# Loading the first half of w_o one block per product, and scaling all of w_ffn_down on VectorE

## The chip, the core and the metric

The kernel runs on one core of one Trainium2 chip. The core has a matrix engine (TensorE; PE in the profile, its weight loads PEld), three engines for elementwise work (VectorE, or DVE; ScalarE, or ACT; GpSimd, or POOL) and SyncE (SP), which here only issues DMAs. Each engine takes its instructions strictly in the order in which they were written, and waits on semaphores for the others. The metric is the device time of one execution in microseconds; the median of several runs is what is compared.

## The reference

One block of a network over 1024 latent tokens of width 1024 and 256 context tokens, batch 1, in fp32: a two-way mLSTM branch and a grouped-query attention branch on the same normed input, their gated merge, and a SwiGLU. Cut to what matters here:

```python
def merge_branches(zg, ym, ya, w_pa, w_pb, w_o):
    g_m, g_a = jnp.split(jax.nn.sigmoid(zg), N_BRANCH, axis=-1)
    return (g_m * (ym @ w_pa) + g_a * (ya @ w_pb)) @ w_o

def swiglu(h, w_g, w_u, w_d):
    return (jax.nn.silu(h @ w_g) * (h @ w_u)) @ w_d

def reference(x, ...):
    ...
    x = x + g1 * y                  # y is merge_branches' result
    x = x + g2 * swiglu(rmsnorm(x, norm2_g[l]) * (1.0 + sc2) + sh2, w_ffn_gate[l], w_ffn_up[l], w_ffn_down[l])
    return rmsnorm(x, final_g)
```

The gates g1 and g2 are vectors over the 1024 output columns. The kernel multiplies them into the columns of w_o and of w_ffn_down.

## The kernel before

Every fp32 product is made from three matmuls (mm3, L104 to L106): each operand is first split into a high part (`split`, L98, ScalarE) and a low part, what the high part leaves (L99, on GpSimd, or on VectorE where the call says so). A block of weights therefore passes a load (L129, issued by SP), in some cases a scaling (L131, VectorE), L98 and L99 before PE can use it.

Buffers of 4 KB per partition ("s" in the profile, and `s_` with a number where instructions are listed) come from one list that hands out the buffer that has been free longest. A load into a buffer waits for the last user of the buffer.

**From w_pb to w_o.** The loop over n (eight, KT) multiplies each 128 columns of w_pb with the attention output, for two halves of the tokens: 24 matmuls to a product. VectorE evicts each product from PSUM (L1426 and L1427; their inputs, the gate and the other branch, are loaded into tile t at L1420 and L1421), and ScalarE and GpSimd split it into mT, the operand of the next products. `load_o(b, js)` loads, scales and splits blocks j of the column half b of w_o. Then come the products with w_o: for two halves of the tokens, two column halves b, four token tiles t, 24 matmuls each. The order of the instructions on every queue is that of the text, except where the scheduler of the program moves an instruction with others of its place. Products have five PSUM banks here.

**Down projection.** w_ffn_down is multiplied in five groups of two blocks, by a Strassen scheme with seven products to a group (`ORDER`: n = 1, 2, 6, 7, 5, 4, 3). Group 0 is a set alone, groups 1 and 2 are the second, 3 and 4 the third set; within a set a product is accumulated in PSUM over its groups, four PSUM banks to a product (q = 0 to 3), eight banks in all. `down_load` issues the loads of a step five steps ahead, `down_prep` makes the operands two steps ahead: the four blocks (a, b) of the weights are scaled by the gate (`scaled`, L1685), combined (`minus`, L1688), and split. When a product is complete, its four banks are evicted, by ScalarE (L1789) for group 0 with n = 1, 6, 7, else by VectorE, which adds to an accumulator (L1791). L1766 adds accumulators at the end.

Of the kernel before, what the change touches and what calls it, by code (L numbers as in the profile page):

```python
# [19 lines left out]
KT = D // P  # L20
# [67 lines left out]
class Block:  # L88
# [1078 lines left out]
    def run(self):  # L1167
        nc, tc, io = self.nc, self.tc, self.io
# [33 lines left out]
        def PS(tags, name):  # L1202

            turn[tags] = i = turn.get(tags, -1) + 1
            tag = tags[i % len(tags)]
            return psum.tile([P, 512], F32, name=name, tag=tag, bufs={"X": 3, "K": 2, "Y": 2, "Z": 1}[tag])
# [15 lines left out]
        slots = self.slots = Slots()  # L1222
# [181 lines left out]
        gbc = slots.get([P, D], F32)  # L1404
        nc.sync.dma_start(gbc, self.d_g[0:1, :].partition_broadcast(P))
        w_o = {}

        def load_o(b, js):

            for j in js:  # L1410
                w_o[b, j] = self.load_s(slots, io["w_o"], 2 * j, 2, b * 512, 512, scale=gbc, lo_eng=nc.gpsimd if j % 2 else nc.vector)

        for n in range(KT):
            if n + 2 < KT:
                w_pb.append(self.load_s(slots, io["w_pb"], 0, KT, (n + 2) * P, P))
            w = w_pb[n]
            for half in range(2):
                hs = slice(half * 512, (half + 1) * 512)
                t = slots.get([P, 2, 512], F32)
                nc.sync.dma_start(t[:, 0], self.d_sm[D + n * P:D + (n + 1) * P, hs])  # L1420
                nc.sync.dma_start(t[:, 1], self.d_ms[n * P:(n + 1) * P, hs])  # L1421
                o = PS(self.acc, "pj")
                for k in range(KT):
                    y = yq[half][k // 2]
                    self.mm3(o, (w[0][:, k], w[1][:, k]), (y[0][:, k % 2], y[1][:, k % 2]), k == 0, k == KT - 1)
                nc.vector.tensor_tensor(t[:, 0], o, t[:, 0], op=ALU.mult)  # L1426
                nc.vector.tensor_tensor(t[:, 0], t[:, 0], t[:, 1], op=ALU.add)  # L1427
                hi, lo = mT[half][n // 2]
                self.split(hi[:, n % 2], lo[:, n % 2], t[:, 0])
                slots.put(t)  # L1430
            slots.put(*w)
            if n >= KT - 2:
                load_o(0, (0, 1) if n == KT - 2 else (2, 3))
        for half in range(2):
            for q in range(4):
                slots.put(*yq[half][q])
# [83 lines left out]
        for half in range(2):  # L1520
# [5 lines left out]
            if not half:  # L1526
                load_o(1, range(4))
# [142 lines left out]
        def down_prep(i, n):  # L1670

            if i == len(groups):
                ops = [slots.get([P, D], F32R) for e in range(4)]
                x, r = down[i, "a", n], down[i, "w", n]
                nc.vector.tensor_tensor(r, r, gbc, op=ALU.mult)
                self.split(ops[0], ops[1], x.rearrange("p a b -> p (a b)"))
                self.split(ops[2], ops[3], r, nc.vector)
                slots.put(x, r)
                down[i, n] = ops
                return  # L1680
            m = len(groups[i])

            def scaled(a, b, eng):
                r = down[i, a, b]
                eng.tensor_tensor(r, r, gbc[:, None, b * 512:(b + 1) * 512].broadcast_to([P, m, 512]), op=ALU.mult)  # L1685

            def minus(out, a, b, eng=nc.vector):
                eng.tensor_tensor(out, a, b, op=ALU.subtract)  # L1688

            if n == 1:  # L1690
                scaled(0, 0, nc.vector)
            elif n == 2:
                scaled(1, 0, nc.gpsimd if i else nc.vector)
            src = {1: (0, 0), 2: (1, 0), 6: (0, 0), 7: "t", 5: (0, 1), 4: (1, 0), 3: (1, 1)}[n]
            r = down[(i, src) if n == 7 else (i,) + src]
            ops = [slots.get([P, m, 512], F32R) for e in range(4)]
            self.split(ops[0], ops[1], down[i, n], nc.gpsimd if i or n not in (1, 6, 7) else nc.vector)
            self.split(ops[2], ops[3], r, nc.vector)
            if n == 2:
                r11, r12, r21, r22 = [down[i, a, b] for a in range(2) for b in range(2)]  # L1700
                scaled(0, 1, nc.vector)
                scaled(1, 1, nc.gpsimd if i else nc.vector)
                t3 = down[i, "t"] = slots.get([P, m, 512], F32)
                minus(t3, r22, r12)
                minus(r12, r12, r11)
                minus(r11, r22, r12)
                minus(r21, r21, r11, nc.gpsimd)
            slots.put(down[i, n])
            if n not in (1, 2):
                slots.put(r)  # L1710
            down[i, n] = ops

        def ahead(k, more=0):

            while at[0] < min(len(seq), k + (LOADS if k >= 0 else 3 + more) + 1):
                down_load(*seq[at[0]])
                at[0] += 1
            while at[1] < min(len(seq), k + PREPS + more + 1):
                down_prep(*seq[at[1]])
                at[1] += 1  # L1720
# [9 lines left out]
        for j in range(FP):  # L1730
# [18 lines left out]
            else:  # L1749
                self.drop_blocks("11", "21")  # L1750
                gbc = slots.get([P, D], F32)
# [141 lines left out]
```

## Time and profile before

| | us |
|---|---|
| median of 3 runs | 2277.96 |
| lowest and highest of the 3 | 2274.88 and 2279.34 |
| the profiled execution | 2284.03 |
| its span | 2282.2 |

The profile is of one execution of its own, 6.07 us above the median. The span is the part of it that the trace covers, from the first instruction to the last. Differences that are worked out from the trace are taken from the span and then set against the median. The granted TensorE clock is given in shares of full speed (2.4 GHz), and was 0.977 as a mean over the span.

### The profile page before, as it was taken

Reading aid. Unit: us, or ns where it says so; the run is one execution under the profiler, and the core shown is the slowest. Engines: PE = TensorE matmul, PEld = TensorE weight load, DVE = VectorE, ACT = ScalarE, POOL = GpSimd, SP = SyncE. Lnnn points to the kernel's source line nnn. Section 1 sums busy time; section 2 is a strip of 40 time slices with the busy share of each in tenths; the row PEclk is TensorE's granted clock in tenths of the full one; section 3 lists DMA queues with packets and bytes.
Section 4 is the critical chain, followed back from the end, with each engine's and each line's share of the span. In section 5 each row is a group of like instructions: output and inputs, shape, how many; then the busy total and the mean of one; then the engine's idle time right before and its main releaser. Section 6 shows DMA issues by size and latency. Waiting matters only on the chain. (4 is left out here: it accounts for less than half of the span.)

```text
span 2282.2 us, 29965 instructions
## 1 busy us (share of the span) xinstructions
PE 2151.4 (94%) x10875; PEld 1779.6 (78%) x10875; DVE 1529.8 (67%) x2771; ACT 980.7 (43%) x1955; POOL 906.1 (40%) x593
## 2 busy tenths in 40 slices
PE   5899999999999899999999999989799999989997
PEld 2698888988887677877877777867588888877885
DVE  4767567477879786876877786245846464667687
ACT  4534434244443564643766764124523232323343
POOL 1422222322323240302655563321554545456875
PEclk9999999999999899999999999999899999999998
DMA  7132333233323822047322224432142323274431
GB/s 263 56 89 91 109 93 106 84 97 111 98 92 105 313 76 86 11 143 254 101 77 86 84 70 137 132 130 82 47 134 94 115 91 117 94 241 144 172 102 74
DMA packets 171632, 262.40 MB, mean 115 GB/s; under 512 B 13326, under 2 KB 111702, under 8 KB 171484
## 3 DMA queue, kind: packets, MB, share of 16 engines
q1 hardware_dynamic: 161564, 236.66, 31.7%
q10 hardware_dynamic: 9920, 23.82, 2.8%
q8 instruction: 86, 1.41, 0.2%
q14 instruction: 62, 0.51, 0.1%
HBM read 190.11 MB, written 70.34 MB: 114 GB/s over the span
## 5 line engine op out<-in xcount | busy, mean ns | idle before, releaser
L99 POOL TENSOR_TENSOR s<-s,s 128x1024 fp32r<-128x1024 f32 (+1 forms) x195 | 403.9, 2084 | 670.5 <-ACT s L98 476.7
L104 PE MATMUL pr<-s,s 128*128 128x512 f32 (+1 forms) x1736 | 621.8, 360 | 19.5 <-DVE s L261 9.8
L98 ACT ACTIVATE s<-s 128x1024 fp32r<-128x1024 f32 (+2 forms) x438 | 359.4, 846 | 633.9 <-DVE s L233 80.4
L105 PE MATMUL pr<-s,s 128*128 128x512 f32 (+1 forms) x1736 | 622.5, 359 | 8.2 <-POOL s L99 5.8
L106 PE MATMUL pr<-s,s 128*128 128x512 f32 (+1 forms) x1736 | 622.1, 359 | 8.4 <-POOL s L99 4.7
L99 DVE TENSOR_TENSOR s<-s,s 128x1024 fp32r<-128x1024 f32 (+2 forms) x243 | 290.3, 1203 | 144.5 <-ACT s L98 109.8
L104 PEld LDWEIGHTS pr<-s,s 128*128 128x128 f32 x1736 | 330.4, 191 | 72.4 <-ACT s L98 13.9
L106 PEld LDWEIGHTS pr<-s,s 128*128 128x128 f32 x1736 | 330.7, 191 | 59.2 <-POOL s L99 6.4
L105 PEld LDWEIGHTS pr<-s,s 128*128 128x128 f32 x1736 | 330.9, 191 | 58.1 <-POOL s L99 6.8
L104 PE MATMUL pj<-s,s 128*128 128x512 f32 x568 | 227.4, 400 | 18.9 <-DVE s L1791 7.9
L105 PE MATMUL pj<-s,s 128*128 128x512 f32 x568 | 225.9, 398 | 4.3 <-DVE s L99 2.2
L106 PE MATMUL pj<-s,s 128*128 128x512 f32 x568 | 225.5, 397 | 1.2 <-POOL s L99 1.2
L261 DVE TENSOR_TENSOR s<-s,pr 128x512 f32<-128x512 f32 x200 | 133.1, 681 | 77.0 <-PE pr L106 72.9
L1566 DVE TENSOR_TENSOR s<-s,pr 128x512 f32<-128x512 f32 x154 | 99.6, 679 | 112.1 <-ACT s L1582 103.8
L104 PEld LDWEIGHTS pj<-s,s 128*128 128x128 f32 x568 | 109.0, 192 | 47.5 <-DVE s L1791 8.7
L1576 POOL TENSOR_TENSOR s<-s,s 128x512 f32<-128x512 f32 x44 | 70.5, 1603 | 167.8 <-ACT s L98 91.1
L1086 DVE TENSOR_TENSOR PT<-pt,PT 128x512 fp32r<-128x512 f32 (+1 forms) x192 | 112.5, 599 | 34.5 <-ACT PT L1085 32.8
L1071 ACT ACTIVATE pr<-sc,st 128x512 f32<-128x512 f32 (+1 forms) x192 | 117.8, 621 | 35.4 <-DVE st L1063 35.4
L362 POOL TENSOR_SCALAR wm<-wm,sc 128x1024 f32<-128x1024 f32 x32 | 91.2, 2849 | 103.0 <-DVE PT L1086 95.5
L105 PEld LDWEIGHTS pj<-s,s 128*128 128x128 f32 x568 | 109.4, 193 | 27.9 <-DVE s L99 3.3
L106 PEld LDWEIGHTS pj<-s,s 128*128 128x128 f32 x568 | 109.2, 192 | 25.1 <-POOL s L99 2.4
L1085 ACT ACTIVATE PT<-pt 128x512 fp32r<-128x512 f32 (+1 forms) x192 | 95.5, 525 | 66.7 <-PE pt L1082 66.0
(316 smaller groups left out, 3622.8 us busy)
## 6 DMA issues: line engine op xcount, KB each, us to landing
s<-in_w_in_dram SPq DMA_DIRECT2D x60, 512.0 KB, 3.7
d_act<-s SPq DMA_DIRECT2D x74, 256.0 KB, 2.0
s<-d_act SPq DMA_DIRECT2D x37, 512.0 KB, 4.6
wm<-in_w_mod_dram SPq DMA_DIRECT2D x32, 512.0 KB, 3.8
s<-in_w_ffn_gate_dram SPq DMA_DIRECT2D x22, 512.0 KB, 4.6
s<-in_w_ffn_up_dram SPq DMA_DIRECT2D x22, 512.0 KB, 3.9
s<-in_w_ffn_down_dram SPq DMA_DIRECT2D x22, 512.0 KB, 8.0
s<-in_w_mod_dram SPq DMA_DIRECT2D x32, 256.0 KB, 4.7
```

What stands on the lines that cost most here:

```text
L98: nc.scalar.activation(hi, src, AF.Copy)
L99: (lo_eng or nc.gpsimd).tensor_tensor(lo, src, hi.bitcast(F32), op=ALU.subtract)
L104: nc.tensor.matmul(out, lhsT=lhs[0], rhs=rhs[0], start=first, stop=False)
L105: nc.tensor.matmul(out, lhsT=lhs[0], rhs=rhs[1], start=False, stop=False)
L106: nc.tensor.matmul(out, lhsT=lhs[1], rhs=rhs[0], start=False, stop=last)
L261: eng.tensor_tensor(out, a, b, op=ALU.add)
L362: x = nc.gpsimd.tensor_scalar(loaded[i], loaded[i], self.sc[:, k, 0:1], None, op0=ALU.mult)
L1071: nc.scalar.activation(pr[:, s0:s0 + n], sc[j][:, 0:n], AF.Exp, bias=st[:, 3:4], accum_out=st[:, 4 + j:5 + j])
L1085: nc.scalar.activation(hi, src, AF.Copy)
L1086: self.pace = nc.vector.tensor_tensor(lo, src, hi.bitcast(F32), op=ALU.subtract)
L1566: nc.vector.tensor_tensor(out, a, b, op=ALU.add)
L1576: nc.gpsimd.tensor_tensor(g, g, o, op=ALU.mult)
```

## The change

It has two parts. First, the four blocks of the first column half of w_o (b = 0) are loaded one after each of the last four steps of the w_pb loop (n = 4, 5, 6, 7), where two came after n = 6 and two after n = 7; and the low parts of two of these blocks (j = 1 and 3) are made by VectorE in place of GpSimd. Second, in groups 1 to 4 of the down projection VectorE also makes the scalings of the blocks (1, 0) and (1, 1), which GpSimd made.

```diff
         def load_o(b, js):
 
             for j in js:
-                w_o[b, j] = self.load_s(slots, io["w_o"], 2 * j, 2, b * 512, 512, scale=gbc, lo_eng=nc.gpsimd if j % 2 else nc.vector)
+                w_o[b, j] = self.load_s(slots, io["w_o"], 2 * j, 2, b * 512, 512, scale=gbc, lo_eng=nc.gpsimd if b and j % 2 else nc.vector)
...
             slots.put(*w)
-            if n >= KT - 2:
-                load_o(0, (0, 1) if n == KT - 2 else (2, 3))
+            if n >= KT - 4:
+                load_o(0, (n - KT + 4,))
...
             elif n == 2:
-                scaled(1, 0, nc.gpsimd if i else nc.vector)
+                scaled(1, 0, nc.vector)
...
                 scaled(0, 1, nc.vector)
-                scaled(1, 1, nc.gpsimd if i else nc.vector)
+                scaled(1, 1, nc.vector)
```

The order of PE's instructions is the same in both kernels. Three places show what moves on the others.

VectorE, in the middle of the w_pb loop (the difference; + is the change, - is before). L1426 and L1427 are evictions: tile s_13718 is that of n = 2 and the second half of the tokens, s_13756 and s_13788 are those of n = 3. L131 and L99 with s_13967, s_13890 and s_13892 are the scalings of w_o's blocks j = 1 and j = 0 and the low part of j = 0; s_14024 is block j = 0 before:

```order
 L1426 TENSOR_TENSOR s_13718<-pj,s_13718 128x512
+L131 TENSOR_TENSOR s_13967<-s_13967,s_13538 128x1024
 L1427 TENSOR_TENSOR s_13718<-s_13718 128x512
 L1426 TENSOR_TENSOR s_13756<-pj,s_13756 128x512
 L1427 TENSOR_TENSOR s_13756<-s_13756 128x512
+L131 TENSOR_TENSOR s_13890<-s_13890,s_13538 128x1024
+L99 TENSOR_TENSOR s_13892<-s_13890,s_13891 128x1024
 L1426 TENSOR_TENSOR s_13788<-pj,s_13788 128x512
 L1427 TENSOR_TENSOR s_13788<-s_13788 128x512
-L131 TENSOR_TENSOR s_14024<-s_14024,s_13538 128x1024
```

Two scalings and a low part now stand ahead of the place where the first scaling stood before; the next two rows of the difference have block j = 2's scaling ahead of the second eviction of n = 4.

VectorE, around the last products with w_pb. First before: s_13992 is n = 6, s_14038 and s_14070 are n = 7; s_14109 is block j = 3 of the first half of w_o, s_14140, s_14147, s_14133 and s_14126 are the second half's:

```order
L1426 TENSOR_TENSOR s_13992<-pj,s_13992 128x512
L1427 TENSOR_TENSOR s_13992<-s_13992 128x512
L131 TENSOR_TENSOR s_14109<-s_14109,s_13538 128x1024
L1426 TENSOR_TENSOR s_14038<-pj,s_14038 128x512
L131 TENSOR_TENSOR s_14140<-s_14140,s_13538 128x1024
L1427 TENSOR_TENSOR s_14038<-s_14038 128x512
L131 TENSOR_TENSOR s_14147<-s_14147,s_13538 128x1024
L99 TENSOR_TENSOR s_14142<-s_14140,s_14141 128x1024
L131 TENSOR_TENSOR s_14133<-s_14133,s_13538 128x1024
L1426 TENSOR_TENSOR s_14070<-pj,s_14070 128x512
```

The same place in the change, where n = 6 is s_13974 and s_14006, and n = 7 is s_14045 and s_14077 (s_14111 is the low part of block j = 3):

```order
L131 TENSOR_TENSOR s_14109<-s_14109,s_13538 128x1024
L1426 TENSOR_TENSOR s_13974<-pj,s_13974 128x512
L1427 TENSOR_TENSOR s_13974<-s_13974 128x512
L99 TENSOR_TENSOR s_14111<-s_14109,s_14110 128x1024
L1426 TENSOR_TENSOR s_14006<-pj,s_14006 128x512
L1427 TENSOR_TENSOR s_14006<-s_14006 128x512
L131 TENSOR_TENSOR s_14133<-s_14133,s_13538 128x1024
L1426 TENSOR_TENSOR s_14045<-pj,s_14045 128x512
L1427 TENSOR_TENSOR s_14045<-s_14045 128x512
```

Block j = 3 stood behind both evictions of n = 6 and now stands ahead of both; between it and the eviction of n = 7 there is one scaling of the second half's (s_14133).

VectorE, at the down projection's second group of weights (the difference; s_18158, s_18106, s_18110 and s_18154 are the blocks (1, 0) and (1, 1) of groups 1 and 2, s_18016 is an accumulator of group 0):

```order
 L1685 TENSOR_TENSOR s_18004<-s_18004,s_17710 128x1024
 L1791 TENSOR_TENSOR s_17918<-pj,s_17918 128x512
+L1685 TENSOR_TENSOR s_18158<-s_18158,s_17710 128x1024
 L1791 TENSOR_TENSOR s_17919<-pj,s_17919 128x512 x2
+L1685 TENSOR_TENSOR s_18106<-s_18106,s_17710 128x1024
 L99 TENSOR_TENSOR s_18117<-s_17720,s_18116 128x1024
 L1685 TENSOR_TENSOR s_18108<-s_18108,s_17710 128x1024
+L1685 TENSOR_TENSOR s_18110<-s_18110,s_17710 128x1024
+L1685 TENSOR_TENSOR s_18154<-s_18154,s_17710 128x1024
 L99 TENSOR_TENSOR s_18166<-s_18004,s_18165 128x1024
 L1791 TENSOR_TENSOR s_18016<-pj,s_18016 128x512
```

Four scalings more now stand on VectorE ahead of the eviction into s_18016. GpSimd has the counterpart (the difference again):

```order
 L99 TENSOR_TENSOR s_18063<-s_17924,s_18062 128x1024
-L1685 TENSOR_TENSOR s_18158<-s_18158,s_17710 128x1024
 L99 TENSOR_TENSOR s_18115<-s_17960,s_18114 128x1024
-L1685 TENSOR_TENSOR s_18106<-s_18106,s_17710 128x1024
-L1685 TENSOR_TENSOR s_18110<-s_18110,s_17710 128x1024
-L1685 TENSOR_TENSOR s_18154<-s_18154,s_17710 128x1024
 L99 TENSOR_TENSOR s_18164<-s_18006,s_18163 128x1024
 L99 TENSOR_TENSOR s_18207<-s_18060,s_18206 128x1024
```

Three scalings in a row stood ahead of the low parts s_18164 and s_18207 there, and are gone. Groups 3 and 4 have the same later.

## Rows read from the trace of the kernel before

**Rows 1.** The page's first part: engine, busy us (share of the span) xinstructions.

```profile
PE 2151.4 (94%) x10875; PEld 1779.6 (78%) x10875; DVE 1529.8 (67%) x2771; ACT 980.7 (43%) x1955; POOL 906.1 (40%) x593
```

**Rows 2.** Windows of three stretches (columns in the first line).

```profile
core 0: us, PE busy (x) PEld busy (x) DVE busy (x) ACT busy (x) POOL busy (x), PEclk, DMA share, GB/s
...
1488.00:1503.00 15.00, 8.31 (x18) 5.18 (x18) 13.07 (x9) 4.49 (x5) 7.89 (x4) 0.66 0.69 259
2050.00:2100.00 50.00, 44.59 (x173) 35.68 (x174) 37.91 (x32) 18.98 (x25) 33.51 (x12) 0.87 0.44 157
2200.00:2240.00 40.00, 36.68 (x149) 28.93 (x148) 35.55 (x25) 11.86 (x13) 39.84 (x13) 0.92 0.15 55
```

**Rows 3.** Timeline of PE: start, us, instruction, [idle before <-releaser].

```profile
1487.78 0.39 PE L106 MATMUL pj<-s,s 128*128 128x512 f32 x1
1492.31 0.64 PE L104 MATMUL pj<-s,s 128*128 128x512 f32 x1 [4.15 <-ACT s L98]
1495.11 0.80 PE L105 MATMUL pj<-s,s 128*128 128x512 f32 x1 [2.16 <-POOL s L99]
...
1505.09 0.39 PE L106 MATMUL pj<-s,s 128*128 128x512 f32 x1
```

**Rows 4.** Timeline of VectorE from the w_pb loop to the first w_o products.

```profile
1435.22 0.69 DVE L1426 TENSOR_TENSOR s<-pj,s 128x512 f32<-128x512 f32 x1 [4.02 <-PE pj L106]
...
1440.66 0.69 DVE L1426 TENSOR_TENSOR s<-pj,s 128x512 f32<-128x512 f32 x1 [3.54 <-PE pj L106]
...
1455.09 1.22 DVE L131 TENSOR_TENSOR s<-s,s 128x1024 f32<-128x1024 f32 x1 [13.01 <-DMA s<-in_w_o_dram]
...
1481.04 1.23 DVE L131 TENSOR_TENSOR s<-s,s 128x1024 f32<-128x1024 f32 x1 [9.18 <-DMA s<-in_w_o_dram]
...
1483.45 1.23 DVE L99 TENSOR_TENSOR s<-s,s 128x1024 fp32r<-128x1024 f32 x1 [0.58 <-ACT s L98]
...
1489.89 1.23 DVE L131 TENSOR_TENSOR s<-s,s 128x1024 f32<-128x1024 f32 x1 [3.52 <-DMA s<-in_w_o_dram]
1491.04 0.68 DVE L1426 TENSOR_TENSOR s<-pj,s 128x512 f32<-128x512 f32 x1
```

**Rows 5.** Timeline of GpSimd and of SyncE's DMA issues, same place.

```profile
1492.34 2.72 POOL L99 TENSOR_TENSOR s<-s,s 128x1024 fp32r<-128x1024 f32 x1 [3.92 <-ACT s L98]
...
1476.04 19.41 SPq L129 DMA_DIRECT2D s<-in_w_o_dram  x5
```

**Rows 6.** Timeline of PE in the down projection.

```profile
2075.64 0.39 PE L106 MATMUL pj<-s,s 128*128 128x512 f32 x1
2081.06 0.80 PE L104 MATMUL pj<-s,s 128*128 128x512 f32 x1 [5.04 <-DVE s L1791]
...
2088.62 0.39 PE L106 MATMUL pj<-s,s 128*128 128x512 f32 x1
```

**Rows 7.** Timeline of VectorE in the down projection.

```profile
2057.57 1.88 DVE L1791 TENSOR_TENSOR s<-pj,s 128x512 f32<-128x512 f32 x3
...
2067.86 2.20 DVE L99 TENSOR_TENSOR s<-s,s 128x1024 fp32r<-128x1024 f32 x1 [3.51 <-issue]
...
2077.06 3.34 DVE L1688 TENSOR_TENSOR s<-s,s 128x1024 f32<-128x1024 f32 x1 [6.41 <-POOL s L99]
2080.33 0.68 DVE L1791 TENSOR_TENSOR s<-pj,s 128x512 f32<-128x512 f32 x1
```

**Rows 8.** Timeline of GpSimd and ScalarE, same stretch and the end.

```profile
2063.22 9.11 POOL L1685 TENSOR_TENSOR s<-s,s 128x1024 f32<-128x1024 f32 x3
2072.30 10.32 POOL L99 TENSOR_TENSOR s<-s,s 128x1024 fp32r<-128x1024 f32 x4
...
2194.49 5.77 POOL L99 TENSOR_TENSOR s<-s,s 128x1024 fp32r<-128x1024 f32 x2 [2.86 <-ACT s L98]
...
2068.26 1.08 ACT L98 ACTIVATE s<-s 128x1024 fp32r<-128x1024 f32 x1
```

**Rows 9.** Instructions of L1685: engine, xcount, duration ns min/median/max, starts.

```profile
L1685 DVE TENSOR_TENSOR s<-s,s x12: 1211/1221/3417, 2011.5 to 2144.0; 128x1024 f32<-128x1024 f32 x12
...
L1685 POOL TENSOR_TENSOR s<-s,s x8: 2388/3379/3409, 2056.6 to 2152.4; 128x1024 f32<-128x1024 f32 x8
```

**Rows 10.** Landing times of the loads of w_ffn_down, and PE's wait near the end.

```profile
DMA to landing us min/median/max: 4.8/8.0/9.1
...
2232.36 0.47 PE L104 MATMUL pj<-s,s 128*128 128x512 f32 x1 [2.14 <-DVE s L1791]
```

## Prediction

> **What bounds the kernel now.** The page's first part comes first: PE is busy 94% of the span, no other engine more than 67% [rows 1]. The time is PE's instructions plus PE's pauses, and a change that gives PE no work and takes none, as here, can only move pauses. So the next view is where PE pauses near the edits, by windows and then by PE's own timeline.
>
> There are three such stretches [rows 2]. From 1488 to 1503 PE is busy 8.31 of 15 us at a granted clock of 0.66, from 2050 to 2100 it is busy 44.59 of 50 at 0.87, from 2200 to 2240 36.68 of 40 at 0.92. The mean clock below 1 says that part of the stretch ran at the lower of TensorE's two levels, 1.2 in place of 2.4 GHz, so a pause costs its length and then the slow matmuls behind it.
>
> What matters first is how fast PE goes undisturbed. Two evictions in a row, each of which waited for PE, start at 1435.22 and 1440.66 [rows 4]: a product of 24 matmuls takes 5.44 us, 0.2267 us to a matmul.
>
> **The first stall.** The second of these evictions is the second half of n = 3. Counting on by 5.44, the first product of n = 7 ends at 1440.66 + 7 x 5.44 = 1478.7, the second at 1484.2. The first product with w_o gets 18 matmuls, three blocks, done by 1488.0; PE then waits 4.15 us for the high part of block j = 3 (ScalarE, L98), and one matmul on 2.16 us for its low part (GpSimd, L99) [rows 3]. What that costs is read from a matmul that runs at full pace again: the 27th after the stop, counting the one at 1492.31 as the first, starts at 1505.09 [rows 3]; undisturbed it would start at 1488.01 + 26 x 0.2267 = 1493.90. The loss is **11.2 us**.
>
> Why is block 3 late? SyncE issued the last loads of w_o from 1476.04 on [rows 5], and VectorE stands in order at the scaling of each: 13.01, 9.18 and 3.52 us of waits for the DMA [rows 4]. The product of n = 7 that PE had finished at 1478.7 was evicted at 1491.04, behind the last of these. The GpSimd low part then takes 2.72 us from 1492.34 [rows 5].
>
> **The change, first part.** The loads now come one for each of n = 4 to 7, and by the order the scaling of block 3 stands ahead of the evictions of n = 6, which PE has ready at 1467.9 and 1473.3 (1440.66 + 5 and 6 x 5.44); its low part stands between the two. Even if the load is issued only when the eviction of the product before, ready at 1462.4, is past (some 1465), lands after 5.0 us as the load issued at 1476.04 did (scaled at 1481.04), and is scaled (1.23), rounded on ScalarE (1.08, the same shape in [rows 8]) and subtracted on VectorE (1.23), it is ready by 1474. An estimate from these rows, but needed only at 1488.0: the margin is 14 us. No PSUM bank is missing meanwhile: VectorE stood still for 13.01 us before 1455.09 and PE ran on.
>
> What is late next? Ahead of the eviction of n = 7, ready at 1478.7, now stands one scaling of the second half's blocks, whose load waits for the buffer that block 3's low part frees, so about 1476 with SyncE's own 2 us. With 5.0 us it lands at 1481, the scaling ends at 1482.3, the two instructions of the eviction at 1483.7 (0.69 each), ScalarE's high part near 1484.3, and GpSimd's low part, behind a 128x1024 low part that can take 2.72, by about 1487.2 to 1488.5. The first w_o product reads it in its 21st matmul, at 1484.2 + 20 x 0.2267 = 1488.7. So it just holds, and this is the thin place: 0 to 4 us of loss may come back. I take 0, since each step of that chain is taken from a disturbed stretch and may only be shorter. Term: **-11.2 us** (bounds -11.2 to -7).
>
> Two low parts move to VectorE: 2 x 1.23 us, beside waits of 13.01 and 9.18 us that now end. They cost nothing; without that cover 2.5 us.
>
> **The second stall.** In the down projection PE stops after the matmul at 2075.64, for 5.04 us, since the next PSUM bank is evicted only by the L1791 at 2080.33 [rows 6, 7]. The 21st matmul starts at 2088.62, undisturbed at 2075.87 + 20 x 0.2267 = 2080.40: **8.2 us** lost. Ahead of that eviction VectorE stood 6.41 us before L1688, for a buffer that a GpSimd low part frees; GpSimd had run three scalings from 2063.22 for 9.11 us, then that low part as the second in a run of four from 2072.30 (10.32, 2.58 each) [rows 7, 8].
>
> **The change, second part.** Eight scalings go from GpSimd to VectorE, four of them here. On GpSimd they took 2.39 to 3.41 us each. On VectorE a scaling takes 1.21 to 3.42 [rows 9], the long ones beside a GpSimd instruction. The high part for that low part starts on ScalarE at 2068.26 and takes 1.08 [rows 8]; then GpSimd, no longer in arrears, frees the buffer at 2069.3 + 2.4 to 3.4 = 71.7 to 72.7 (all from 2000). So GpSimd is no more the last; VectorE is. Its queue, walked from the L1791 at 57.57: one eviction to 58.2; first new scaling beside GpSimd's low part, 3.42, to 61.6; two evictions to 62.9; second new scaling alone, 1.22, to 64.1; a low part to 65.3; the old scaling, alone now, to 66.5; the third and fourth new one beside GpSimd's next low parts, 3.42 each, to 73.3; a low part of 2.20 (that at 2067.86) to 75.5; an eviction to 76.1; L1688, between 1.21 and 3.34, to 78.4; and the eviction that PE waits for ends at 79.1. It ended at 81.0 before. So the stall gets 1.9 us shorter and does not go: PE still needs the bank at 75.87, and the pause of some 3 us is above the 2.14 after which PE slowed near the end [rows 10]. I take **-2 us**. Bounds: none of the four contended gives the whole -8.2 (VectorE is then at L1688 when the buffer is free, at 71.7, and PE's bank is ready at 73.6). All four contended and nothing of the waits used adds 13.7 - 6.41 = +7.3.
>
> What the trace shows here is contention: the same scaling takes 1.21 alone and 3.42 beside GpSimd, whose own takes 2.39 alone and up to 3.41 [rows 9]. The Trainium skill, in "SBUF — State Buffer", section "SBUF: two separate sides", says that VectorE with two SBUF inputs and GpSimd take turns at one port pair, each holding it for a whole instruction. The trace agrees: 3.42 is near the 1.21 + 2.39 of one behind the other. By the rule the stall stays for the most part, without it the sum would have -8.2 in place of -2.
>
> For groups 3 and 4 the same four scalings stand ahead of evictions and wait for loads, which land a median of 8.0 us after issue, 9.1 at most [rows 10]. The last of them began at 2152.4 on GpSimd [rows 9]; with 1.22 for it and 0.68 for the eviction behind it that bank is free at 2154.3. The second set begins near 2088.2, with [rows 6]; PE needs that bank after twelve products of 5.44 and 18 matmuls more (4.1), at 2157.6. With 3.3 us of slack I charge 0 (bound +4).
>
> **The end.** From 2200 to 2240 GpSimd is busy 39.84 of 40 us [rows 2], in arrears since 2194.49 [rows 8], and PE pauses there 3.32 us and loses up to 0.08 x 36.68 = 2.9 by the clock. GpSimd has no scalings left there, so the change only reaches it through an earlier start: PE comes earlier as well, so most stays. I take **-1** (bounds -6.2 and +4, as in groups 3 and 4).
>
> **The sum.** -11.2 - 2 - 1 = -14.2. Against the profiled span, 2282.2 gives 2268.0; that execution was 6.07 us above the median, so the comparison goes to the median: 2277.96 - 14.2 = 2263.8, rounded to **2264 us**.
>
> **Rivals.** B: the down projection gains nothing, since VectorE with four more instructions ends where GpSimd did, and the end neither. For it speaks that VectorE is the busier of the two (67% against 40%), and that all of its contention stays: 2277.96 - 11.2 = 2266.8. The Trainium skill's "Perfetto Trace Analysis", section "Optimizing Scalar/DVE Operations", warns of this: work moved between VectorE and GpSimd may not help, as they share a port. The trace agrees in part; GpSimd's 9.11 us in a row become at most 3.42 each on VectorE.
> C: half of the first stall comes back, through the low part of n = 7 that has 0 to 1.5 us of margin: +5.6 on mine, 2269.4. For it speaks the thin margin, against it that VectorE is out of its arrears by then.
> D: all three stalls go, for which VectorE has to run its scalings alone: -11.2 - 8.2 - 6.2 = -25.6, 2252.4. Against it speaks GpSimd at 33.51 of 50 us in that window.
> E, slower: in groups 3 and 4 VectorE, which alone evicts, stands before a scaling whose load is late. One place, the last load's scaling: each microsecond beyond the 3.3 us of slack goes to PE. To use up 14.2 and 4.6 more it would have to begin 22.1 us after 2152.4, which is more than twice the slowest landing, 9.1: the place is real, the size unlikely. At that point it gives 2282.6.
> F: nothing that can be measured, within 0.2% (4.6 us, 2273.4 to 2282.5, about what a measurement of this kernel can tell from no change): the first stall is taken over by another wait of the same size, as by an x load that a buffer holds back; 2278.
>
> **How the numbers follow.** Chances: mine 0.48 (its own range 2260 to 2267), B 0.16, C 0.12, D 0.10, F 0.09, E 0.05. The range 2252 to 2271 holds mine, B, C and about half of D. Faster 0.86, same 0.09, slower 0.05.
>
> **What would show it.** From 1400 to 1510 no PE wait over 1 us and a granted clock near 1.00; block 3's scaling on VectorE near 1470. L1685 on VectorE 20 times, on GpSimd none. The second stall, some 11 us earlier in time, still there with 3 to 4 us of pause before L1791, with VectorE busy without a break ahead of it, not waiting for GpSimd. The end still has PE waits for L1791. I am wrong if VectorE waits for a DMA at L131 or L1685 while PE waits for VectorE.

## The result, and the profile after

| | before | after |
|---|---|---|
| median of 9 runs, us | 2277.96 | 2267.21 |
| lowest and highest, us | 2269.34, 2281.53 | 2256.80, 2270.89 |
| span of the profiled execution, us | 2282.2 | 2262.3 |

The ratio of the runs is 0.9938, 95% interval 0.9924 to 0.9953: of 2277.96 us that is 14.1 us less (10.7 to 17.3). The ratio is not the quotient of the two medians: these differ by 10.75 us, at the lower end of that interval. Forecast were 14.2 less and 2264 us, 3.2 us under the median. The gains in us of the experiments below are worked out from the ratios in the same way.

The page's first part: PE's share is what it was, GpSimd has lost 30 us of work and VectorE gained 7, though it runs ten instructions more ([rows 1]); so the others take less time than before.

```profile
PE 2137.3 (94%) x10875; PEld 1772.1 (78%) x10875; DVE 1536.5 (68%) x2781; ACT 981.7 (43%) x1955; POOL 876.3 (39%) x583
```

The three stretches in windows (columns as in [rows 2]; the later ones start 10 us earlier, as PE does):

```profile
1488.00:1503.00 15.00, 14.39 (x63) 11.93 (x64) 8.70 (x7) 4.47 (x6) 4.25 (x3) 1.00 0.55 192
2040.00:2090.00 50.00, 45.89 (x197) 36.56 (x197) 45.73 (x40) 19.30 (x25) 23.62 (x9) 1.00 0.46 163
2190.00:2230.00 40.00, 37.03 (x159) 29.34 (x158) 37.68 (x26) 4.86 (x5) 35.21 (x12) 1.00 0.04 17
```

The granted clock is 1.00 in all three, where it was 0.66, 0.87 and 0.92. The second pair is not quite like with like. Before, the window opens inside another stall: PE waits 4.10 us at 2049.86 for a bank that ScalarE evicts (L1789), and its matmuls are slow up to 2056. The change has this stall too (4.18 us), but at 2037.48, ahead of its window. A window before that begins behind it has 0.93 and 186 matmuls; PE's wait before, then that window:

```profile
2049.86 0.80 PE L104 MATMUL pj<-s,s 128*128 128x512 f32 x1 [4.10 <-ACT s L1789]
```

```profile
2056.00:2106.00 50.00, 44.59 (x186) 35.91 (x185) 38.84 (x33) 17.67 (x22) 35.92 (x13) 0.93 0.38 133
```

In the second and third PE is busy hardly longer than before (45.89 against 44.59 of 50, 37.03 against 36.68 of 40), but executes more matmuls in that time (197 against 173, 159 against 149).

**The first stall.** PE's timeline at the first product with w_o:

```profile
1486.96 0.39 PE L105 MATMUL pj<-s,s 128*128 128x512 f32 x1
1488.61 0.50 PE L106 MATMUL pj<-s,s 128*128 128x512 f32 x1 [1.26 <-POOL s L99]
```

The waits for block 3 ([rows 3]) are gone; one wait of 1.26 us stands in their place, for the low part of mT of n = 7. VectorE ahead of it, then GpSimd and SyncE's issue:

```profile
1472.87 1.23 DVE L131 TENSOR_TENSOR s<-s,s 128x1024 f32<-128x1024 f32 x1 [5.49 <-DMA s<-in_w_o_dram]
...
1477.49 1.23 DVE L99 TENSOR_TENSOR s<-s,s 128x1024 fp32r<-128x1024 f32 x1 [2.07 <-POOL s L99]
...
1482.48 1.23 DVE L131 TENSOR_TENSOR s<-s,s 128x1024 f32<-128x1024 f32 x1 [2.44 <-DMA s<-in_w_o_dram]
1483.63 0.69 DVE L1426 TENSOR_TENSOR s<-pj,s 128x512 f32<-128x512 f32 x1
```

```profile
1484.94 3.61 POOL L99 TENSOR_TENSOR s<-s,s 128x1024 fp32r<-128x1024 f32 x2 [2.87 <-ACT s L98]
...
1478.74 0.38 SPq L129 DMA_DIRECT2D s<-in_w_o_dram  x1
```

Block 3 is scaled at 1472.87, and its low part, which waits 2.07 us for a low part on GpSimd, ends at 1478.72. The second half's block, whose load SyncE issues at 1478.74 after waiting for this low part, is scaled at 1482.48, ahead of the eviction of n = 7; its low part is the first of the two on GpSimd that end at 1488.55, and the second is the one that PE waits for.

**The down projection.** PE's waits (the first is the one that the kernel before has as well), VectorE's timeline, and L1685's instructions (as [rows 6, 7, 9]):

```profile
2037.48 0.79 PE L104 MATMUL pj<-s,s 128*128 128x512 f32 x1 [4.18 <-ACT s L1789]
2049.38 0.51 PE L104 MATMUL pj<-s,s 128*128 128x512 f32 x1 [1.69 <-DVE s L1791]
2065.30 0.50 PE L104 MATMUL pj<-s,s 128*128 128x512 f32 x1 [0.69 <-DVE s L1791]
2068.62 0.50 PE L104 MATMUL pj<-s,s 128*128 128x512 f32 x1 [1.67 <-DVE s L1791]
```

```profile
2045.89 2.83 DVE L1685 TENSOR_TENSOR s<-s,s 128x1024 f32<-128x1024 f32 x1
2048.65 1.27 DVE L1791 TENSOR_TENSOR s<-pj,s 128x512 f32<-128x512 f32 x2
...
2052.11 3.48 DVE L1685 TENSOR_TENSOR s<-s,s 128x1024 f32<-128x1024 f32 x3
...
2061.25 3.40 DVE L1688 TENSOR_TENSOR s<-s,s 128x1024 f32<-128x1024 f32 x1 [1.71 <-POOL s L99]
2064.57 0.68 DVE L1791 TENSOR_TENSOR s<-pj,s 128x512 f32<-128x512 f32 x1
```

```profile
L1685 DVE TENSOR_TENSOR s<-s,s x20: 1205/1213/2834, 1999.0 to 2134.1; 128x1024 f32<-128x1024 f32 x20
```

The wait of 5.04 us has become 0.69 and 1.67, and a wait of 1.69 has come ahead of it. Three of the scalings in a row take 3.48 us, so 1.2 each; only the first new one, at 2045.89, took 2.83, and the eviction behind it is what PE waits for at 2049.38.

**The end.** PE's waits there:

```profile
2213.81 0.50 PE L106 MATMUL pj<-s,s 128*128 128x512 f32 x1 [0.26 <-POOL s L99]
2215.49 0.50 PE L104 MATMUL pj<-s,s 128*128 128x512 f32 x1 [0.48 <-DVE s L1791]
2218.82 0.49 PE L104 MATMUL pj<-s,s 128*128 128x512 f32 x1 [1.67 <-DVE s L1791]
...
2227.84 0.47 PE L104 MATMUL pj<-s,s 128*128 128x512 f32 x1 [0.55 <-DVE s L1791]
```

**Losses.** For each run the same sum is made from PE's timeline: over a stall, the distances between the starts of matmuls less 0.2267 us each, from the last matmul at full pace before it to the first after it. It is a pause and its slow matmuls together. "First" is the start of the w_o products, "ahead" the wait that is at 2049 in the change, "second" the stall of the down projection, "end" the waits before the last products (two to four). The last four columns are of one profiled execution each. The stall at 2049.86 before and 2037.48 in the change is not in the table: every kernel has it, at 4.7 to 7.2 us (7.1 before, 5.8 in the change).

| kernel | ratio (95% interval) | first | ahead | second | end |
|---|---|---|---|---|---|
| before | 1 | 11.2 | 0 | 8.2 | 6.7 |
| the change | 0.9938 (0.9924 to 0.9953) | 1.5 | 2.0 | 2.9 | 4.0 |
| w_o part alone | 0.9967 (0.9955 to 0.9979) | 6.8 | 0 | 8.4 | 6.7 |
| down projection alone | 0.9963 (0.9950 to 0.9977) | 11.2 | 2.0 | 2.8 | 4.3 |
| early loads alone | 0.9970 (0.9959 to 0.9981) | 5.8 | 3.7 | 6.4 | 7.0 |
| low parts alone | 0.9995 (0.9983 to 1.0006) | 10.7 | 0 | 9.5 | 6.9 |
| groups 1, 2 only | 0.9958 (0.9942 to 0.9975) | 1.4 | 2.0 | 2.9 | 6.9 |
| groups 3, 4 only | 0.9953 (0.9940 to 0.9967) | 6.8 | 0 | 8.3 | 4.1 |
| block (1, 0) only | 0.9960 (0.9947 to 0.9972) | 3.9 | 0 | 4.7 | 7.0 |
| one step earlier | 0.9927 (0.9908 to 0.9946) | 0 | 2.0 | 2.9 | 3.8 |
| ... and one scaling back | 0.9917 (0.9896 to 0.9938) | 0 | 0 | 6.3 | 1.6 |
| ... and four sums moved | 0.9941 (0.9922 to 0.9961) | 0 | 2.1 | 2.8 | 9.6 |

### The profile page after: what moved, and what is told of

It is laid out like the page before. It is cut to its first block, busy times and chain, and to the rows that moved or that the text cites. A ratio compares the mean times of both kernels' runs of the same rounds, so it can differ in the third digit from the quotient of the medians.

```text
span 2262.3 us, 29955 instructions
## 1 busy us (share of the span) xinstructions
PE 2137.3 (94%) x10875; PEld 1772.1 (78%) x10875; DVE 1536.5 (68%) x2781; ACT 981.7 (43%) x1955; POOL 876.3 (39%) x583
## 5 line engine op out<-in xcount | busy, mean ns | idle before, releaser
L99 POOL TENSOR_TENSOR s<-s,s 128x512 fp32r<-128x512 f32 (+1 forms) x193 | 398.2, 2075 | 693.8 <-ACT s L98 446.7
L99 DVE TENSOR_TENSOR s<-s,s 128x1024 fp32r<-128x1024 f32 (+2 forms) x245 | 291.3, 1197 | 144.5 <-ACT s L98 110.8
L104 PE MATMUL pj<-s,s 128*128 128x512 f32 x568 | 223.2, 393 | 13.1 <-DVE s L1791 6.8
L105 PE MATMUL pj<-s,s 128*128 128x512 f32 x568 | 222.1, 391 | 1.6 <-DVE s L99 1.6
L106 PE MATMUL pj<-s,s 128*128 128x512 f32 x568 | 222.1, 391 | 1.5 <-POOL s L99 1.5
L104 PEld LDWEIGHTS pj<-s,s 128*128 128x128 f32 x568 | 107.0, 188 | 39.9 <-DVE s L1791 8.8
L105 PEld LDWEIGHTS pj<-s,s 128*128 128x128 f32 x568 | 107.0, 188 | 24.3 <-DVE s L99 2.7
L106 PEld LDWEIGHTS pj<-s,s 128*128 128x128 f32 x568 | 106.9, 188 | 24.3 <-POOL s L99 2.4
```

What stands on the lines that cost most here:

```text
L99: (lo_eng or nc.gpsimd).tensor_tensor(lo, src, hi.bitcast(F32), op=ALU.subtract)
L104: nc.tensor.matmul(out, lhsT=lhs[0], rhs=rhs[0], start=first, stop=False)
L105: nc.tensor.matmul(out, lhsT=lhs[0], rhs=rhs[1], start=False, stop=False)
L106: nc.tensor.matmul(out, lhsT=lhs[1], rhs=rhs[0], start=False, stop=last)
```

## The experiments

**The w_o part alone** (the w_o lines as in the change, the scalings as before).

```diff
-                scaled(1, 0, nc.vector)
+                scaled(1, 0, nc.gpsimd if i else nc.vector)
...
-                scaled(1, 1, nc.vector)
+                scaled(1, 1, nc.gpsimd if i else nc.vector)
```

> Only the w_o part of the change; the down projection as before. My theory: the two parts do not touch each other. The stall at the first w_o product shrinks from 11.2 us to about 1.5 as in the full change, the stall of the down projection stays near 8.2 and that near the end near 6.7, so the time is about 10 us (0.9956) under before. Rival: the first part carries everything and the later stalls only shrank because PE met the other engines in another phase; then it is about 14 us (0.994) under before and the later stalls are small here too.

2274.7 us against 2283.28, ratio 0.9967: 7.5 us (4.8 to 10.3). The two later stalls are as before, so the rival falls. But the first stall is 6.8 us and not 1.5 in the profiled execution (2280.43 us, 5.7 above the median of its kernel, while that of the change was 3.1 under its own), with the same instructions in the same order up to there. PE, VectorE, GpSimd and SyncE's issue in this run:

```profile
1492.02 0.50 PE L104 MATMUL pj<-s,s 128*128 128x512 f32 x1 [0.42 <-ACT s L98]
...
1495.83 0.79 PE L106 MATMUL pj<-s,s 128*128 128x512 f32 x1 [3.08 <-POOL s L99]
```

```profile
1478.34 1.22 DVE L131 TENSOR_TENSOR s<-s,s 128x1024 f32<-128x1024 f32 x1 [6.64 <-DMA s<-in_w_o_dram]
...
1488.75 1.23 DVE L131 TENSOR_TENSOR s<-s,s 128x1024 f32<-128x1024 f32 x1 [3.24 <-DMA s<-in_w_o_dram]
```

```profile
1491.20 4.57 POOL L99 TENSOR_TENSOR s<-s,s 128x1024 fp32r<-128x1024 f32 x2 [3.67 <-ACT s L98]
...
1484.21 0.38 SPq L129 DMA_DIRECT2D s<-in_w_o_dram  x1
```

The last matmul ahead of the first wait is 1492.02 - 0.42 - 0.39 = 1491.2 here; the same one was two matmuls ahead of 1486.96 in the change, at 1486.5. So PE is 4.7 us later. VectorE waits 6.64 us for the load of block 3, against 5.49. The second half's block, issued at 1484.21, is scaled 4.54 us later, against 3.74 in the change; the two low parts take 4.57 us and not 3.61. The low part that PE needs ends at 1495.8, not 1488.6: 7.2 us later where PE is 4.7 later, and PE waits 0.42 and 3.08. Of the loss of 6.8, 3.5 is pause and 3.3 the slow matmuls behind it.

**The down projection alone** (the loads and low parts of w_o as before).

```diff
-                w_o[b, j] = self.load_s(..., lo_eng=nc.gpsimd if b and j % 2 else nc.vector)
+                w_o[b, j] = self.load_s(..., lo_eng=nc.gpsimd if j % 2 else nc.vector)
...
-            if n >= KT - 4:
-                load_o(0, (n - KT + 4,))
+            if n >= KT - 2:
+                load_o(0, (0, 1) if n == KT - 2 else (2, 3))
```

> Only the scalings of the down projection on VectorE; the w_o part as before. My theory: the first stall stays at 11.2 us, the stall of the down projection shrinks by some 5 us, a new wait of about 2 us stands before it, the end gains 2 to 3: in sum 4 to 7 us under before (0.998). Rival: nothing is gained here, the ratio is 1.000 within 0.001, and the later stalls are as large as before.

2273.42 us against 2283.28, ratio 0.9963: 8.4 us (5.2 to 11.4), more than the 4 to 7 that were expected, though 7 lies in the interval. The first stall is 11.2, the later ones are those of the change. The rival "nothing gained here" falls. The two parts sum to 15.9 where 14.1 were measured together, which agrees within the intervals: the runs show no effect of one part on the other's stalls.

**The two halves of the w_o part.** Early loads with GpSimd's low parts, and the old loads with VectorE's, the down projection as before in both:

```diff
-                w_o[b, j] = self.load_s(..., lo_eng=nc.gpsimd if j % 2 else nc.vector)
+                w_o[b, j] = self.load_s(..., lo_eng=nc.gpsimd if b and j % 2 else nc.vector)
```

(that is the second; the first has only the loads at n = 4 to 7).

> Only the loads of w_o's first half at n = 4 to 7; the low parts of blocks 1 and 3 stay on GpSimd, the down projection as before. If the place of the loads is what counts, the first stall falls to about 2 us and the time is 9 to 10 us under before (0.996). If the engine of the low parts counts as much, GpSimd's low part of block 3 or of n = 7 is late, and at least 4 of the 11.2 us stay.

> Only the low parts of blocks 1 and 3 of w_o's first half on VectorE; the loads where they were, the down projection as before. If the place of the loads is what counts, PE still waits for ScalarE's high part of block 3 for some 4 us and then for the low part: 0 to 3 us are gained (0.999 to 1.000), or something is lost where the low part stands behind a scaling that waits for its DMA. If the engine of the low parts counts, 5 us or more are gained.

2275.41 us (0.9970) and 2280.74 us (0.9995, not to be told from 1). The place of the loads is the part that counts; moving the low parts alone does nothing that can be measured. In the first PE waits 0.61 and 3.07 us, as with the whole w_o part: not for a low part of block 3 but for the parts of n = 7. So at least 4 us stay, as in the expectation's second case; but the engine of block 3's low part is not the reason, since the w_o part alone, which has it on VectorE, keeps the same waits.

**Which scalings.** GpSimd gets the scalings of groups 3 and 4 back (`i > 2`), or those of groups 1 and 2 (`i in (1, 2)`), or block (1, 1)'s in all four:

```diff
-                scaled(1, 0, nc.vector)
+                scaled(1, 0, nc.gpsimd if i > 2 else nc.vector)
...
-                scaled(1, 1, nc.vector)
+                scaled(1, 1, nc.gpsimd if i > 2 else nc.vector)
```

> The full change, but in groups 3 and 4 the scalings of blocks (1, 0) and (1, 1) go back to GpSimd; groups 1 and 2 have them on VectorE. My theory: the stall of the down projection near 2065 is as small as in the change (2.9 us, not 8.2), while the stall near the end is as large as before (about 6.7, not 4.0), so the time is about 2 to 3 us over the full change, ratio near 0.995. Rival: the stall near the end is set by the instructions there and the phase of PE; then it is 4.0 here too.

> The full change, but in groups 1 and 2 the scalings of blocks (1, 0) and (1, 1) go back to GpSimd; groups 3 and 4 have them on VectorE. My theory: the stall of the down projection is back at about 8 us and the new wait of about 2.3 us ahead of it is gone, the stall near the end is 3 to 4 us; ratio near 0.995. Rival: the stall of the down projection comes from VectorE's own queue and stays near 3 us.

> The full change, but the scalings of block (1, 1) go back to GpSimd in groups 1 to 4, so VectorE has four scalings more than before and not eight. My theory: the new wait of about 2.3 us near 2049, behind the scaling of a block (1, 1) on VectorE, is gone; the two scalings on GpSimd still stand ahead of the low part that frees VectorE's buffer, so some 2 us of the old 8.2 us stall come back on the 2.9 that the change left: the time is that of the full change within 2 us. Rival: any scaling on GpSimd there brings the whole stall of 8 us back, and the time is 3 us or more over the full change.

2269.57, 2269.97 and 2271.42 us against 2281.28. The table shows the split as it was expected: with groups 1 and 2 alone the second stall is 2.9 and the end 6.9, with groups 3 and 4 alone 8.3 and 4.1. PE at the end in the first of these runs, and PE and VectorE at the second stall in the second:

```profile
2216.00 0.47 PE L104 MATMUL pj<-s,s 128*128 128x512 f32 x1 [2.16 <-DVE s L1791]
```

```profile
2072.14 0.80 PE L104 MATMUL pj<-s,s 128*128 128x512 f32 x1 [6.06 <-DVE s L1791]
```

```profile
2068.14 3.35 DVE L1688 TENSOR_TENSOR s<-s,s 128x1024 f32<-128x1024 f32 x1 [6.34 <-POOL s L99]
```

Each is the wait of the kernel before again ([rows 6, 7, 10]). With block (1, 0) only on VectorE, the wait ahead is gone and the second stall 4.7 us, about what both are together in the change (4.9); but the end is back at 7.0, which the expectation did not have. The ratio of 0.9960 is 5 us above the change's, not within 2 us, though the intervals overlap.

**One step earlier.** The change with w_o's first half at n = 3 to 6:

```diff
-            if n >= KT - 4:
-                load_o(0, (n - KT + 4,))
+            if KT - 5 <= n < KT - 1:
+                load_o(0, (n - KT + 5,))
```

> The full change with the loads of w_o's first half one step earlier still, at n = 3 to 6. By the order of the instructions no load of the second half then stands ahead of the eviction of n = 7 on VectorE, nor its low part ahead of that of n = 7 on GpSimd. My theory: what is left of the first stall (1.5 us in the change, 6.8 with the first part alone, though both have the same instructions there) is that place alone; here it is under 0.5 us and the time is 1 to 4 us under the change, ratio 0.992 to 0.993. Rival: an earlier load only takes buffers from tiles and x loads, another wait of the same size stands there, and the ratio is that of the change or worse.

2262.64 us, ratio 0.9927. There is no wait of PE at the w_o products. A window over them, then VectorE and GpSimd:

```profile
1470.00:1500.00 30.00, 30.00 (x134) 24.86 (x133) 15.15 (x14) 8.30 (x14) 7.62 (x4) 1.00 0.46 160
```

```profile
1470.60 0.69 DVE L1426 TENSOR_TENSOR s<-pj,s 128x512 f32<-128x512 f32 x1 [3.55 <-PE pj L106]
...
1475.25 2.56 DVE L131 TENSOR_TENSOR s<-s,s 128x1024 f32<-128x1024 f32 x2 [3.23 <-DMA s<-in_w_o_dram]
```

```profile
1472.76 1.29 POOL L99 TENSOR_TENSOR s<-s,s 128x512 fp32r<-128x512 f32 x1 [3.68 <-ACT s L98]
```

The eviction of n = 7 is now released by PE and no load stands before it; its low part is ready at 1474.05, and is first read by the 24th matmul of the product that starts at 1470.60 + 5.44 = 1476.0, at 1481.2. That leaves 7 us. The two runs below have the same order there and no wait either, while the five profiles with the order of the change all have one: it is a matter of order. Against the change, whose interval overlaps, the gain is not settled by times.

**One scaling back**, on top of this: block (1, 1) of group 2, which stands ahead of an eviction.

```diff
-                scaled(1, 1, nc.vector)
+                scaled(1, 1, nc.gpsimd if i == 2 else nc.vector)
```

> The kernel with w_o's loads at n = 3 to 6 and all scalings on VectorE, but one scaling goes back to GpSimd: block (1, 1) of group 2, the one that stands ahead of an eviction on VectorE. My theory: the wait of 1.7 us for L1791 near 2045 is gone, the two waits near 2060 stay at 0.7 and 1.7, and the time is some 2 us under that of the kernel without this step. Rival: the scaling on GpSimd delays the low part that frees VectorE's buffer, and the stall near 2060 grows by as much or more. The first w_o product starts without a wait in this run too, if its wait was a matter of order; if it was luck in one execution, 1 to 6 us of it are back.

2264.65 us, ratio 0.9917; the step itself is within the noise of the kernel that it builds on. The wait ahead is gone, but the second stall has grown from 2.9 to 6.3. PE and VectorE:

```profile
2066.00 0.50 PE L104 MATMUL pj<-s,s 128*128 128x512 f32 x1 [1.92 <-DVE s L1791]
2069.31 0.79 PE L104 MATMUL pj<-s,s 128*128 128x512 f32 x1 [1.28 <-DVE s L1791]
```

```profile
2061.94 3.40 DVE L1688 TENSOR_TENSOR s<-s,s 128x1024 f32<-128x1024 f32 x1 [1.70 <-POOL s L99]
```

VectorE waits for GpSimd's buffer as long as in the change (1.70, 1.71) and its L1688 takes as long (3.40): the low part was not delayed. PE came to the same bank earlier (its wait begins 2.1 us after this L1688 starts, in the change 3.4) and waited there, so the wait was moved, and the clock fell behind it. Theory and rival both miss this; the stall grew as the rival said, for another reason. That the end loses less here (1.6 for 3.8) may come from PE's later arrival; no run shows it.

**Four sums moved** at the end, on top of the loads one step earlier:

```diff
-                for x, y, eng in {2: ((2, 1, nc.gpsimd),), 6: ((6, 1, nc.gpsimd),), ...
+                for x, y, eng in {2: ((2, 1, nc.vector),), 6: ((6, 1, nc.vector),), ...
```

> The kernel with w_o's loads at n = 3 to 6 and all scalings on VectorE, and four additions of accumulators near the end (products 2 and 6 with 1) go from GpSimd to VectorE. My theory: what is left of the stall near the end, some 3.8 us in two places, is GpSimd's arrears and the turns that VectorE and GpSimd take; four additions of 2.4 us or more become four of 1.2 us, and the stall falls to under 2 us, the time by about 2. Rival: VectorE, which evicts, is the bound there; with four additions more it evicts later and the stall grows to 5 us or more.

2269.34 us, ratio 0.9941, and the end is 9.6 us: in the profile the rival is right, while the ratio's interval overlaps that of the kernel that this one builds on. PE, VectorE and GpSimd:

```profile
2218.73 0.77 PE L104 MATMUL pj<-s,s 128*128 128x512 f32 x1 [3.51 <-DVE s L1791]
```

```profile
2208.00 3.35 DVE L99 TENSOR_TENSOR s<-s,s 128x1024 fp32r<-128x1024 f32 x1
2211.28 3.42 DVE L1766 TENSOR_TENSOR s<-s,s 128x1024 f32<-128x1024 f32 x1
2214.61 3.37 DVE L99 TENSOR_TENSOR s<-s,s 128x1024 fp32r<-128x1024 f32 x1
2217.91 0.68 DVE L1791 TENSOR_TENSOR s<-pj,s 128x512 f32<-128x512 f32 x1
```

```profile
2207.86 9.04 POOL L99 TENSOR_TENSOR s<-s,s 128x1024 fp32r<-128x1024 f32 x3 [3.21 <-ACT s L98]
```

Three instructions of VectorE take 3.4 us each, beside three low parts of GpSimd, ahead of the eviction that PE waits for. At the end VectorE's queue is the bound, not GpSimd's arrears as such.

## Why the prediction was right

The total was right, 14.2 forecast and 14.1 (10.7 to 17.3) measured, and so was the mechanism; the terms were not sized right, and their errors cancel. That the total agrees to 0.1 us is luck. Measured alone, the first part gives 7.5 us (4.8 to 10.3) where 11.2 were forecast, and the second 8.4 (5.2 to 11.4) where 3 were.

**The first stall, forecast -11.2.** In five profiled executions with the change's order there, the loss left was 1.4, 1.5, 3.9, 6.8 and 6.8 us. The step that failed is "so it just holds": the low part of n = 7, forecast ready by 1487.2 to 1488.5 and needed at 1488.7, kept PE waiting 1.26 us in the change and 3.08 in the run of its first part. Place, chain and wait were those that the step names, and its bound of 4 us was too small, since it left out the slow matmuls. The chain went wrong at its first link: block 3's low part, forecast ready by 1474, ended at 1478.72 in the change, since its load came later and VectorE waited for GpSimd in front of it; the next load was issued at once, without the "SyncE's own 2 us", for which no row stands. The low part of n = 7 was then ready at 1488.55, near the end of what was forecast, but PE was some 2 us earlier than in the profile from which the forecast counts. One reading of the step was wrong the other way: the matmul that waits is the 24th of the product, not the 21st, which gave 0.7 us more. Rival C, half of the stall (5.6), lies within what such executions show. That the rest hangs on this place is shown by the kernel with the loads one step earlier. The sign of being wrong came in part: VectorE waited 2.44 us for a DMA at L131 ahead of the eviction of n = 7, and PE's wait behind it, 1.26 us, was over the 1 us that was to be the most.

That the waits for block 3 go is right: its scaling was forecast near 1470 and came at 1472.87. Rival F, another wait of the same size and nothing that can be measured, fell. That the low parts are free on VectorE is in line with the run that moves only them.

**The second stall, forecast -2.** The stall went from 8.2 to 2.9, but 2.0 us stand ahead as a new wait; together -3.3 (-3.3 to -3.4 in four more runs with the scalings of groups 1 and 2 on VectorE, -1.9 in the one with a scaling back). The window from 2050 to 2100, by which the prediction sees this stall, also holds the slow matmuls of the stall at 2049.86, which it does not name. Three steps of the walk failed. The third and fourth new scaling were priced at 3.42 each beside GpSimd's low parts; they ran almost alone, three scalings in 3.48, GpSimd's next low part starting only at 2054.80, when the last of them was under way. And the eviction behind the first new scaling, whose contended price was right in kind (2.83 for 3.42), was not checked against PE's need: it is the wait at 2049. (Such a wait is not the change's alone: with early loads only it is there too, where VectorE's scaling at 2047.49 met one on GpSimd and took 3.38.) "GpSimd is no more the last" was wrong too: L1688 still waited 1.71 us for its low part. The rule of the Trainium skill that was weighed ("SBUF — State Buffer", "SBUF: two separate sides") is in line with the 3.4 us instructions of the last experiment; it said nothing on how many of them would meet, which is what the walk had to find. Rival B fell: the down projection alone gained 8.4 us. The warning of the Trainium skill that goes with it ("Perfetto Trace Analysis", "Optimizing Scalar/DVE Operations"), that such a move might not help, did not come true here, since seven of the eight scalings moved took 1.2 us each on VectorE, and it is in line with the four sums moved at the end, which lengthened the stall.

The pause of some 3 us, forecast as "above the 2.14 after which PE slowed", did not come in one piece: after pauses of 0.69 and 1.67 us the clock stayed at 1.00, and this is part of the gain.

**The end, forecast -1.** It is 2.7 us here, and is shown to come from the scalings of groups 3 and 4 (3.8 to 4.3 with them, 6.7 to 7.0 without or with block (1, 0) only, while the end was otherwise left alone). Rival E, a late load behind which evictions queue, showed nothing: in the change PE waits nowhere between 2130 and 2175.

**Rival D**, that all three go, did not come; the second and the end keep a good half of their losses.

The rest of the 19.9 us between the two profiled spans is not the change's: its stretch up to 1430 was already some 2 us shorter (eviction at 1427.83 for one that [rows 4] put at 1435.22 - 5.44 = 1429.8), and the stall at 2049.86, with a wait ahead of it, cost some 1.9 us less, within the scatter of this stall among the kernels.

## What to carry to other kernels

When a load is brought forward, the next load behind it in the same queues takes its place: look for what that one now stands in front of, and price its delay with the slow matmuls behind the pause. Of a chain that does not hang on PE, a pause that is taken away ahead of it can come back at the next bank, as it did here when one scaling went back; judge such a step by the sum over both. And before an instruction is priced as contended, find out from the trace what the other engine runs in that very microsecond, since here that decided between 1.2 and 3.4 us.

## What was not expected of the hardware

The clock. A pause of 1.69 us and, 16 us later, two of 0.69 and 1.67 left the granted clock at 1.00, as the window shows; pauses of 5.04 and of 3.08 us were followed by matmuls at half pace. With 1.92 and 1.28 us it fell as well: the matmul after the second took 0.79 us and not 0.39. The length of a pause alone does not decide: one of 1.84 us (early loads alone, at 2051.52) and one of 2.10 us (block (1, 0) only, at 1491.09) were followed by matmuls 0.43 us apart instead of 0.23, the ones of 1.67 and 1.69 us were not. The same order of instructions thus costs 1.5 or 6.8 us, by a difference of some 2.5 us in when the low part of n = 7 is ready against when PE wants it; DMA landing and contention make up most of it.
